# Two more MLP features as seven half-size products, and block masks by iota, in a two-layer encoder on one Trainium2 core

## The chip, the cores and the metric

The kernel runs on one core of a Trainium2 chip. The core has five engines that run side by side, each taking its own instructions in order: TensorE (PE in the profile; its weight loads are listed apart as PEld), VectorE (DVE), ScalarE (ACT), GpSimd (POOL) and SyncE (SP). They wait for each other through semaphores. Matrix products land in PSUM banks, everything else lives in SBUF. Loads are issued from the queue of SP, and some adding transfers from the queue of POOL; sixteen DMA engines move the data.

The metric is the device time of one execution, in microseconds. Smaller is better.

## The reference

The program is a two-layer encoder trunk on 512 tokens of width 1024, all in float32. Layer 0 mixes tokens with a bidirectional gated DeltaNet, layer 1 with a bidirectional gated linear attention (GLA). After each mixer and after each MLP the residual is normalised:

```python
for i in range(DEPTH):                       # DEPTH = 2
    m = _mixer_gdn(x, ...) if i == 0 else _mixer_gla(x, ...)
    x = _layernorm(ALPHA * x + m, ln1_g[i], ln1_b[i])
    x = _layernorm(ALPHA * x + _sq_relu_mlp(x, mlp_w1[i], mlp_w2[i]), ln2_g[i], ln2_b[i])

def _sq_relu_mlp(h, w1, w2):                 # w1: 1024 x 4096, w2: 4096 x 1024
    a = jax.nn.relu(jnp.matmul(h, w1))
    return jnp.matmul(a * a, w2)
```

The change touches the MLP, which is run twice, and the masks that the GLA layer uses to pick, level by level, which blocks of a score matrix come from which product.

## The kernel before

Every float32 operand of a large product is split into a high part `h` (a cast, on ACT, line 102) and a low part `l` (a subtraction, on DVE, line 107), and a product is three matmuls: high by high, high by low, low by high (lines 128 to 130). So every weight tile of 128 x 1024 costs one ACT cast and one DVE subtraction before PE can use it. The tiles are `wst` (as loaded), `wh` and `wl` (split); `wst` and the pair `wh`/`wl` are rings of three buffers each. A load can start when the split of the tile three places earlier is done, and a split can start when PE is done with the tile three places earlier.

The 4096 hidden features of the MLP form four groups of eight tiles of 128 features, here called features 1 to 8 of a group (the code counts from 0). The first product (with `w1`) makes a group's features, the second (with `w2`) adds a group's contribution to the output.

- **Group 0, features 1 to 4** (`proj_halves`): four full products, in two halves of 256 tokens.
- **Group 0, features 5 to 8** (`feature`): four full products of 512 tokens, 24 matmuls each.
- **Groups 1 to 3** (`Pair`): two features at a time. A 2 x 2 block product (two halves of the 1024 inputs by two halves of the tokens, for two features) is computed from seven half-size products instead of eight (a Strassen scheme), 12 matmuls of 256 tokens each. That needs sums of weight halves (line 464, DVE, and a half-size split, lines 470 and 471) and sums of token blocks of x (`x_blocks`, lines 433 to 442, then four more splits `xh3`, `xh5`, `xh6`, `xh7`). The x sums are made once for each MLP and used by all pairs.
- **The second product** (`second`) uses the same scheme with seven products for each group, in 28 pieces (`chunks`) of six matmuls of 512 columns. Its weight tiles are `w2r` (as loaded, eight buffers), `w2h` and `w2l`.

A pair's life: `begin` loads its two weight tiles t0 and t1 into `wst`; `prepare` splits t0 for products 1 and 2, forms the sums and splits half of one for product 5; `finish` (`late(0, ...)`) splits the rewritten t0 for products 6 and 4; `late(1, ...)` splits t1 for products 7 and 3, after the pair's second product. PE runs the products in the order 1, 2, 6, 5, 7, 3, 4. They accumulate in two PSUM banks, `fx` and `fyz`; these are the two buffers of the tag `pj`, which features 5 to 8 use too. Between the products ACT and DVE copy or add parts of the banks into the features `h`, and a product that adds to a bank waits until that copy has read it.

In groups 1 to 3 PE's order is written out by hand (`in_order`): pieces of the second product of group g stand between the products of the pairs of group g + 1. The order on DVE, ACT, POOL and SP is set by a scheduler, from priorities and its own estimate of when things end. The queues are then fixed: an instruction that waits holds up everything behind it on its engine.

The masks (`sel_masks`) are seven 128 x 128 tiles of bytes, made once, on POOL, during the first MLP: a memset, two selections, a subtraction and a cast for each level. They are first needed by the GLA layer. The line numbers of the profile are those of this kernel.

## Time and profile before

| what | value |
|---|---|
| median of the runs shown | 1311.15 us (1310.5 to 1313.33, 3 runs) |
| the profiled execution's own time | 1311.28 us |
| its span in the trace | 1309.6 us |
| PE busy | 1289.4 us, 98% of the span |
| DVE busy | 1106.3 us, 84% |
| ACT busy | 804.8 us, 61% |
| POOL busy | 134.6 us, 10% |
| features 5 to 8 of group 0, first MLP | 431.92 to 453.97 us on PE |
| features 5 to 8 of group 0, second MLP | 1005.01 to 1027.09 us on PE |

How to read it: a matmul's row gives its start and its length, but matmuls overlap, so what one costs is the distance from one start to the next. The same holds on DVE and ACT, where one instruction begins shortly before the one ahead of it has ended. "Idle before" in square brackets is the time that an engine stood still before an instruction, with what released it.

### The profile page before, as it was taken

Reading aid. Unit: us, or ns where it says so; the run is one execution under the profiler, and the core shown is the slowest. Engines: PE = TensorE matmul, PEld = TensorE weight load, DVE = VectorE, ACT = ScalarE, POOL = GpSimd, SP = SyncE. Lnnn points to the kernel's source line nnn. Section 1 sums busy time; section 2 is a strip of 40 time slices with the busy share of each in tenths; the row PEclk is TensorE's granted clock in tenths of the full one; section 3 lists DMA queues with packets and bytes.
Section 4 is the critical chain, followed back from the end, with each engine's and each line's share of the span. In section 5 each row is a group of like instructions: output and inputs, shape, how many; then the busy total and the mean of one; then the engine's idle time right before and its main releaser. Section 6 shows DMA issues by size and latency. Waiting matters only on the chain.

```text
span 1309.6 us, 22228 instructions
## 1 busy us (share of the span) xinstructions
PE 1289.4 (98%) x8586; PEld 1106.3 (84%) x8586; DVE 1106.3 (84%) x1795; ACT 804.8 (61%) x1604; POOL 134.6 (10%) x190
## 2 busy tenths in 40 slices
PE   8999999999999999999999999999999999999996
PEld 6778888788878899999998888888888899999985
DVE  7888888988868998999989697877888789989987
ACT  5767676677543656666657754564456566666656
POOL 5000000000003710101102100000000001101021
PEclk9999999999999999999999999999999999999998
DMA  5333313233332664576647521211316376556565
GB/s 191 99 106 96 98 55 108 81 114 96 114 110 84 175 172 169 119 203 161 177 145 154 140 97 56 74 62 52 103 59 218 87 210 165 142 176 139 171 143 144
DMA packets 47805, 165.92 MB, mean 127 GB/s; under 512 B 5923, under 2 KB 6611, under 8 KB 47699
## 3 DMA queue, kind: packets, MB, share of 16 engines
q1 hardware_dynamic: 33603, 114.52, 25.8%
q0 software_dynamic: 13984, 49.95, 18.7%
q8 instruction: 67, 1.10, 0.3%
q14 instruction: 39, 0.32, 0.1%
q10 hardware_dynamic: 112, 0.03, 0.0%
HBM read 125.00 MB, written 2.65 MB: 97 GB/s over the span
## 4 chain that ended last, share of the span: by engine, by line
PE 91%; ACT 3%; DVE 3%; issue 1%; DMA 1%; SPq 0%; DVEq 0%; ACTq 0%
PE pjv L128 3%; PE pjv L129 3%; PE pjv L130 3%; PE pX L130 3%; PE pX L129 3%; PE fx L130 3%; PE fx L128 3%; PE fx L129 3%; PE pX L128 3%; PE m L1776 3%; PE fyz L128 3%; PE fyz L130 3%; PE fyz L129 3%; PE pY L129 2%; PE pY L130 2%; PE pY L128 2%
## 5 line engine op out<-in xcount | busy, mean ns | idle before, releaser
L102 ACT CAST wh<-wst 128x1024 fp32r<-128x1024 f32 x151 | 158.5, 1050 | 104.8 <-PE fyz L129 28.2
L107 DVE TENSOR_TENSOR wl<-wst,wh 128x1024 fp32r<-128x1024 f32 x149 | 183.2, 1232 | 40.3 <-ACT wh L102 40.2
L107 DVE TENSOR_TENSOR w2l<-w2r,w2h 128x1024 fp32r<-128x1024 f32 x92 | 111.5, 1222 | 21.6 <-ACT w2h L102 21.6
L102 ACT CAST w2h<-w2r 128x1024 fp32r<-128x1024 f32 x94 | 98.4, 1048 | 42.5 <-DMA w2r<-w2r 22.8
L415 POOL DMA_DIRECT2D w2r<-w2r x56 | 47.9, 887 | 492.9 <-DVE w2l L107 388.0
L464 DVE TENSOR_TENSOR wst<-wst 128x512 f32<-128x512 f32 x120 | 80.0, 687 | 0.8
L102 ACT CAST ah<-h 128x1024 fp32r<-128x1024 f32 x56 | 58.8, 1050 | 30.6 <-PE pY L129 12.0
L107 DVE TENSOR_TENSOR al<-h,ah 128x1024 fp32r<-128x1024 f32 x56 | 68.4, 1221 | 6.6 <-ACT ah L102 6.6
L130 PE MATMUL pX<-w2h,al 128*128 128x512 f32 x168 | 66.3, 394 | 0.0
L129 PE MATMUL pX<-w2l,ah 128*128 128x512 f32 x168 | 65.9, 392 | 0.0
L128 PE MATMUL pX<-w2h,ah 128*128 128x512 f32 x168 | 65.5, 390 | 0.0
L128 PE MATMUL pjv<-wh,xth 128*128 128x512 f32 x128 | 54.7, 428 | 0.0
L130 PE MATMUL fyz<-xh,wl 128*128 128x256 f32 x192 | 53.5, 278 | 0.0
L130 PE MATMUL fx<-xth,wl 128*128 128x256 f32 x192 | 53.4, 278 | 0.0
L128 PE MATMUL fyz<-xh,wh 128*128 128x256 f32 x192 | 53.4, 278 | 0.0
L128 PE MATMUL fx<-xth,wh 128*128 128x256 f32 x192 | 53.2, 277 | 0.0
L130 PE MATMUL fx<-xh,wl 128*128 128x256 f32 x192 | 53.2, 277 | 0.0
L129 PE MATMUL fx<-xtl,wh 128*128 128x256 f32 x192 | 53.2, 277 | 0.0
L129 PE MATMUL fyz<-xl,wh 128*128 128x256 f32 x192 | 53.1, 277 | 0.0
L129 PE MATMUL fx<-xl,wh 128*128 128x256 f32 x192 | 53.1, 277 | 0.0
L128 PE MATMUL fx<-xh,wh 128*128 128x256 f32 x192 | 53.1, 277 | 0.0
L129 PE MATMUL pj<-xtl,wh 128*128 128x256 f32 (+1 forms) x160 | 52.0, 326 | 0.2 <-DVE xtl L194 0.2
(542 smaller groups left out, 4312.7 us busy)
## 6 DMA issues: line engine op xcount, KB each, us to landing
wst<-in_w SPq DMA_DIRECT2D x68, 512.0 KB, 4.6
w2r<-in_w SPq DMA_DIRECT2D x60, 512.0 KB, 4.6
w2r<-w2r POOLq DMA_DIRECT2D x56, 512.0 KB, 5.7
wst<-in_a_in SPq DMA_DIRECT2D x31, 512.0 KB, 4.1
wst<-in_b_vr SPq DMA_DIRECT2D x16, 512.0 KB, 3.3
wst<-in_a_out SPq DMA_DIRECT2D x8, 512.0 KB, 4.6
wst<-in_b_in SPq DMA_DIRECT2D x8, 512.0 KB, 3.4
wst<-in_b_out SPq DMA_DIRECT2D x8, 512.0 KB, 3.2
```

The lines of the kernel that those rows point to most:

```text
L102: h = nc.scalar.copy(hi, src)
L107: self.halves = h, nc.vector.tensor_tensor(lo, src, hi.bitcast(F32), ALU.subtract)
L128: mm(ps, ah, bh, start=start, stop=False, **kw)
L129: mm(ps, ah, bl, start=False, stop=False, **kw)
L130: self.last_mm = mm(ps, al, bh, start=False, stop=stop, **kw)
L415: nc.gpsimd.dma_start(blocks[a + (q,)], blocks[b + (q,)], accum_op=ALU.add)
L464: plus = lambda a, b: V.tensor_tensor(a, a, b, ALU.add)
L1776: T.matmul(ps[:, d, :], *ops(d), start=True, stop=True)
```

## The change

Three edits.

1. **Features 7 and 8 of group 0** are made as a pair, by the seven half-size products, in both MLPs. The x sums and their splits, which stood from feature 6 on, are asked for from feature 5 on. Nothing of the second product stands between this pair's products: they follow each other directly on PE. PE's written-out order starts at this pair and runs to the end of the MLP's last group. All later pairs move up by one place in the list `todo`.
2. **The masks** are made from iotas on POOL (one of 128 x 7, seven of 128 x 128) and comparisons on DVE (six shifts and a cast on 128 x 7, seven comparisons of 128 x 128). They move from the start of the first MLP to the end of its first round of groups. A mask of level k now marks every pair of positions that lies in different blocks of 2^k, not only those that first part at this level; the copies under the masks run from the finest level to the coarsest, and a later one overwrites an earlier one.
3. Two tiny memsets allocate the `w2h` and `w2l` rings at the place in the code where they were allocated before, so that the tiles' addresses stay what they were.

```diff
-        todo = [(gi, p) for gi in range(1, G) for p in range(GF // 2)]
+        todo = [(0, GF // 2 - 1)] + [(gi, p) for gi in range(1, G) for p in range(GF // 2)]
...
-        for f in range(4, GF):
+        def step(i, n):
+            if n == 0:
+                begin(i + 1)
+            elif n == 1:
+                ready[i].late(1, (7, 3))
+            elif n == 3:
+                prepare(i + 1)
+            elif n == 5:
+                finish(i + 1)
+
+        for f in (4, 5):
             feature(0, f, h)
-            if f >= 5:
-                next(xb)
-            if f == 4:
-                load(0, 0, 0)
-            if f == 5:
-                load(0, 0, 1)
-            if f == 6:
-                load(0, 1, 1)
-                with tc.issue_after(c.last_hi.ins), tc.issue_after(c.last_lo.ins):
-                    split(1)
-                a = pair(quarters(h)[0])
+            next(xb)
+            load(0, 0, f - 4)
         begin(0)
+        for name in RING["w2"][:2]:
+            V.memset(pool.tile([P, 2, 512], F32R, name=name, tag=name, bufs=3)[:, 0, 0:8].bitcast(F32), 0.0)
+        next(xb)
         prepare(0)
         finish(0)
-        if extra:
-            extra(lambda: pool.tile([P, P], F32, name="tmp", tag="tmp", bufs=2))
+        load(0, 1, 1)
+        with tc.issue_after(c.last_hi.ins), tc.issue_after(c.last_lo.ins):
+            split(1)
+        a = pair(quarters(h)[0])
+        whole = contextlib.ExitStack()
+        whole.enter_context(c.in_order(mybir.EngineType.PE))
+        for n, _ in enumerate(ready[0].products(h)):
+            step(0, n)
...
             h, a = nh, stream.a
+            if extra and gi == 0:
+                with tc.issue_after(c.halves[1].ins):
+                    extra(lambda: pool.tile([P, P], F32, name="tmp", tag="tmp", bufs=2))
...
 def sel_masks(c, pool, tmp):
...
+    G.iota(pi, pattern=[[0, n]], base=0, channel_multiplier=1)
+    for k in range(1, n):
+        V.tensor_scalar(pi[:, k:k + 1], pi[:, k:k + 1], k, None, ALU.arith_shift_right)
+    V.tensor_copy(pf, pi)
...
+    for k in range(n):
+        w = 1 << k
+        f = tmp()
+        G.iota(f.rearrange("p (a b) -> p a b", b=w), pattern=[[1, P // w], [0, w]], base=0, channel_multiplier=0,
+               allow_small_or_imprecise_dtypes=True)
+        m = out[w if k else 0] = pool.tile([P, P], mybir.dt.uint8, name=f"mu{w}", tag=f"mu{w}", bufs=1)
+        V.tensor_scalar(m, f, pf[:, k:k + 1], None, ALU.not_equal if k else ALU.is_equal)
```

On PE the order of all other matmuls stays as it was: in each MLP 48 matmuls of 512 columns go, and 84 of 256 come in their place. On the other engines the scheduler moved more. Three places matter.

**DVE, first MLP, the end of the preparation for the first pair.** In these rows `xl6`, `xl7` and `xl3` are splits of x sums, `wst_6052` is t0 and `wst_6054` is t1 of the first pair of group 1. The last row is the split for that pair's products 6 and 4. Before:

```order
L107 TENSOR_TENSOR xl6_6041<-w2r_5934,xh6_6040 128x1024
L107 TENSOR_TENSOR xl7_6045<-w2r_5938,xh7_6044 128x1024
L107 TENSOR_TENSOR xl3_6049<-w2r_5936,xh3_6048 128x1024
L107 TENSOR_TENSOR wl_6057<-wst_6052,wh_6056 128x1024
L464 TENSOR_TENSOR wst_6052<-wst_6052,wst_6054 128x512
L464 TENSOR_TENSOR wst_6054<-wst_6054 128x512
L464 TENSOR_TENSOR wst_6052<-wst_6052 128x512
L464 TENSOR_TENSOR wst_6052<-wst_6052,wst_6054 128x512
L107 TENSOR_TENSOR w2l_6150<-w2r_6135,w2h_6149 128x1024
L471 TENSOR_TENSOR wl_6064<-wst_6052,wh_6063 128x512
L464 TENSOR_TENSOR wst_6052<-wst_6052,wst_6054 128x512
L107 TENSOR_TENSOR wl_6070<-wst_6052,wh_6069 128x1024
```

Now, where `wst_5950` and `wst_5952` are t0 and t1 of the new pair (features 7 and 8 of group 0):

```order
L107 TENSOR_TENSOR xl6_5965<-w2r_5897,xh6_5964 128x1024
L107 TENSOR_TENSOR xl3_5973<-w2r_5899,xh3_5972 128x1024
L464 TENSOR_TENSOR wst_5950<-wst_5950,wst_5952 128x512
L107 TENSOR_TENSOR w2l_5998<-w2r_5905,w2h_5997 128x1024
L464 TENSOR_TENSOR wst_5952<-wst_5952 128x512
L464 TENSOR_TENSOR wst_5950<-wst_5950 128x512
L471 TENSOR_TENSOR wl_5984<-wst_5950,wh_5983 128x512
L464 TENSOR_TENSOR wst_5950<-wst_5950,wst_5952 128x512 x2
L107 TENSOR_TENSOR w2l_6002<-w2r_5907,w2h_6001 128x1024
L107 TENSOR_TENSOR al_6008<-h_5652,ah_6007 128x1024
L107 TENSOR_TENSOR wl_5990<-wst_5950,wh_5989 128x1024
```

The first split of the second product's weights (`w2l_5998`, `w2l_6002`) and of its left operand (`al_6008`) stood ahead of the rows shown before; they stand between the pair's own sums and its last split now.

**ACT, the same place.** `pj_5907` is feature 6 before, `w2h_6149` the cast of a later `w2` tile, and `wh_6069` the cast for products 6 and 4. Before:

```order
L383 ACTIVATE h_5653<-pj_5907 128x512
L384 ACTIVATE h_5653<-h_5653 128x512
L102 CAST w2h_6149<-w2r_6135 128x1024
L470 CAST wh_6063<-wst_6052 128x512
L383 ACTIVATE h_5653<-pj_5952 128x512
L384 ACTIVATE h_5653<-h_5653 128x512
L102 CAST wh_6069<-wst_6052 128x1024
```

Now, where `pj_5915` is feature 6 and `fx_6011` the first bank of the new pair:

```order
L470 CAST wh_5983<-wst_5950 128x512
L102 CAST w2h_6153<-w2r_6139 128x1024
L383 ACTIVATE h_5653<-pj_5915 128x512
L102 CAST wh_5989<-wst_5950 128x1024
L384 ACTIVATE h_5653<-h_5653 128x512
L499 COPY h_5653<-fx_6011 128x256
L102 CAST wh_6043<-wst_5952 128x1024
```

The cast of the later `w2` tile now stands ahead of the activation of feature 6, which empties the bank that the pair's second product needs. In the second MLP the same cast stands ahead of the activation of feature 5, and the cast for products 6 and 4 ahead of that of feature 6.

**DVE, first MLP, where the masks are made now.** These rows stand where the second product passes from group 0 to group 1; `wl_7030` is the split for products 7 and 3 of a pair. The comparisons for `mu32` and `mu64` follow within four more rows.

```order
L799 TENSOR_SCALAR pi_6923<-pi_6923 128x1 x6
L577 TENSOR_TENSOR h_6133<-h_6134,h_6133 128x4x256
L800 CAST pf_6924<-pi_6923 128x7
L107 TENSOR_TENSOR al_6984<-h_6134,ah_6983 128x1024
L503 TENSOR_TENSOR h_6967<-h_6967,fyz_6998 128x256
L808 TENSOR_SCALAR mu1_6935<-tmp_6933,pf_6924 128x128
L808 TENSOR_SCALAR mu2_6939<-tmp_6937,pf_6924 128x128
L107 TENSOR_TENSOR wl_7030<-wst_6760,wh_7029 128x1024
L808 TENSOR_SCALAR mu4_6943<-tmp_6941,pf_6924 128x128
L808 TENSOR_SCALAR mu8_6947<-tmp_6945,pf_6924 128x128
L107 TENSOR_TENSOR w2l_6992<-w2r_6975,w2h_6991 128x1024
L808 TENSOR_SCALAR mu16_6951<-tmp_6949,pf_6924 128x128
```

Before, no mask instruction stood on DVE. On POOL two of the iotas stay at the start of the MLP and five move behind the twelfth adding transfer of this MLP.

54 lines of the change are left out of this document (15 added, 39 removed).

## The prediction

> **What bounds the kernel now.** I read the busy shares and the chain of waits first, then the windows of the stage that the change touches.
>
> ```profile
> PE 1289.4 (98%) x8586; PEld 1106.3 (84%) x8586; DVE 1106.3 (84%) x1795; ACT 804.8 (61%) x1604; POOL 134.6 (10%) x190
> PE 91%; ACT 3%; DVE 3%; issue 1%; DMA 1%; SPq 0%; DVEq 0%; ACTq 0%
> 431.92:442.95 11.03, 11.03 (x51) 9.06 (x50) 11.03 (x10) 8.27 (x11) 10.20 (x13) 1.00 0.42 142
> 442.95:453.97 11.02, 11.02 (x49) 9.03 (x48) 9.95 (x11) 4.83 (x7) 7.67 (x9) 1.00 0.87 250
> 1005.01:1016.05 11.04, 11.04 (x50) 9.04 (x49) 6.79 (x6) 6.01 (x8) 1.70 (x2) 1.00 1.03 360
> 1016.05:1027.09 11.04, 11.04 (x49) 9.03 (x48) 6.33 (x8) 4.91 (x8) 0.00 (x0) 1.00 0.54 120
> ```
>
> The last four rows are features 5 and 6, then 7 and 8, of the first and of the second MLP: length, then the busy time of PE, PEld, DVE, ACT and POOL, the granted clock, the DMA share and GB/s. PE never stands still in them, at full clock, so fewer matmuls shorten these stretches as long as PE still never waits. DVE is as full as PE in the first MLP (11.03 of 11.03, 9.95 of 11.02) and has room in the second (6.79 and 6.33 of 11.04). So the question is whether the two stages can prepare a pair in time.
>
> **The matmuls: a gain of 2.95 us.** The starts on PE:
>
> ```profile
> 431.92 0.40 PE L128 MATMUL pj<-xth,wh 128*128 128x512 f32 x1
> ...
> 453.97 0.39 PE L128 MATMUL pX<-w2h,ah 128*128 128x512 f32 x1
> ...
> 455.36 0.28 PE L128 MATMUL fx<-xth,wh 128*128 128x256 f32 x1
> ...
> 456.72 0.28 PE L128 MATMUL fyz<-xth,wh 128*128 128x256 f32 x1
> ...
> 458.09 0.39 PE L128 MATMUL pX<-w2h,ah 128*128 128x512 f32 x1
> ...
> 1005.01 0.40 PE L128 MATMUL pj<-xth,wh 128*128 128x512 f32 x1
> ...
> 1027.09 0.39 PE L128 MATMUL pX<-w2h,ah 128*128 128x512 f32 x1
> ```
>
> Features 5 to 8 take 453.97 − 431.92 = 22.05 us, so two of them 11.03; in the second MLP 22.08, so 11.04. One half-size product takes 1.36 or 1.37 us (455.36 to 456.72 to 458.09), a mean of 1.365, so seven take 9.555. Each MLP saves 1.47 or 1.485 us, together 2.95.
>
> A rule speaks against that. The Trainium skill, TensorE: Matmul & The Clock Gate, section Back-to-back issue gap, gives a sustained spacing of about 81 ns for 128 columns and 131 ns for 512, so that narrow matmuls lose. An estimate by that page: 48 x 131 = 6.3 us go and at least 84 x 81 = 6.8 us come, a loss. The rows above do not agree (22.05 us / 96 = 230 ns for 512 columns, 1.365 us / 12 = 114 ns for 256, the same for each column).
>
> **First MLP: DVE comes too late by 1.6 us.** Before, the first pair's product 6 had two pieces of the second product between it and its preparation. Now the pair starts at 431.92 + 11.03 = 442.95, products 1 and 2 take 2.73, and the third matmul of product 6 needs the last DVE split of the new order on DVE (`wl_5990`): 442.95 + 2.73 + 2 x 0.114 = 445.9. When is it done?
>
> ```profile
> 421.94 1.22 DVE L433 TENSOR_TENSOR w2r<-xth,xtl 128x1024 f32<-128x1024 f32 x1
> ...
> 435.79 1.48 DVE L441 SCALAR_TENSOR_TENSOR w2r<-w2r 128x1024 f32<-128x1024 f32 x1
> ...
> 988.92 1.22 DVE L433 TENSOR_TENSOR w2r<-xth,xtl 128x1024 f32<-128x1024 f32 x1
> ...
> 1009.36 1.21 DVE L107 TENSOR_TENSOR xl<-w2r,xh 128x1024 fp32r<-128x1024 f32 x1
> ...
> 1019.81 2.75 DVE L464 TENSOR_TENSOR wst<-wst 128x512 f32<-128x512 f32 x4
> ...
> 545.86 1.29 DVE L464 TENSOR_TENSOR wst<-wst 128x512 f32<-128x512 f32 x2
> ```
>
> DVE can start the x sums at 421.94, when the last part of x is there, as before. From there to `wl_5990` DVE's queue now has 19 instructions of 1024 columns and six of 512. The second MLP shows the price with POOL quiet: from 988.92 to 1009.36 are 18 steps without a gap, 1.136 us each (in the first MLP, beside the masks on POOL, such an instruction took up to 1.48 instead of 1.22; those masks are gone). The 512-wide ones take 0.64 (1.29 / 2) to 0.69 (2.75 / 4) by their lengths. So the end is at 421.94 + 18 x 1.136 + 1.22 + 6 x 0.64 to 0.69 = 447.4 to 447.75, if nothing on DVE waits. PE waits 1.5 to 1.85 us; with one or two short waits of DVE for ACT inside this walk, or the 512-wide ones at the closer spacing that back-to-back rows hide, 1.3 to 2.0. I take 1.6. This eats the first MLP's 1.47.
>
> **ACT ahead of the banks: 0.2 and 0.4 us.** In both MLPs the pair's casts now stand directly before the activations and copies that free a bank.
>
> ```profile
> 450.27 1.05 ACT L102 CAST w2h<-w2r 128x1024 fp32r<-128x1024 f32 x1 [5.16 <-DMA w2r<-in_w]
> ...
> 1016.33 1.05 ACT L102 CAST w2h<-w2r 128x1024 fp32r<-128x1024 f32 x1 [3.67 <-DMA w2r<-in_w]
> 1017.28 1.04 ACT L102 CAST wh<-wst 128x1024 fp32r<-128x1024 f32 x1
> 1018.24 0.59 ACT L383 ACTIVATE h<-pj 128x512 f32<-128x512 f32 x1
> ```
>
> Second MLP: the cast for products 6 and 4 needs feature 6's weight buffer, free at 1016.05; it ends at 1017.1, and the activation of feature 6 behind it at 1017.7. Product 2 wants that bank at 1016.05 + 1.365 = 1017.4: 0.3 us late. Product 3 waits for a copy behind another cast for about 0.1. The split itself is done by 1017.1 + 1.22 = 1018.3, and product 6 needs it at 1016.05 + 2.96 = 1019.0: no wait there, and DVE is free by then (988.92 + 25.8 = 1014.7). So the second MLP keeps 1.485 − 0.4 = 1.1 us. In the first MLP the same copies cost about 0.2.
>
> **Loads.** The next pair's t1 can be loaded only when t0's buffer is free, that is after `wl_5990` (447.5), and DVE wants it at about 452.7, when product 7 is done (447.5 + 1.1 + 2 x 1.365 = 451.3) and a split and an addition behind it: 5.2 us. In the second MLP: 1018.3 to 1024.5, 6.2 us. Issues and landings:
>
> ```profile
> w2r<-in_w SPq DMA_DIRECT2D x4, 512.0 KB, 4.9
> ...
> w2r<-in_w SPq DMA_DIRECT2D x4, 512.0 KB, 8.7
> ...
> 443.63 2.79 SPq L52 DMA_DIRECT2D w2r<-in_w  x3
> ...
> 1008.33 2.60 SPq L52 DMA_DIRECT2D w2r<-in_w  x2
> ```
>
> The first two rows are the median landing times from 425 to 460 and from 995 to 1035. 4.9 us fits, 8.7 would not; in the second MLP 8.7 went with two adding transfers at the same time (DMA share 1.03 above), and these now start later, behind the moved `w2l` splits. I take 0.2 us for the first MLP, none for the second; the far end is 8.7 in both: 3.5 and 2.5 us.
>
> **Masks: 0.3 us.** On POOL a mask cost, before, two selections, a subtraction and a cast, off the path:
>
> ```profile
> L796 POOL TENSOR_SCALAR_AFFINE_SELECT tmp<-tmp 128x128 f32<-128x128 f32 x7 | 7.9, 1134 | 0.3
> ...
> 409.91 0.15 DVE L206 TENSOR_SCALAR rst<-rst 128x1 f32<-128x1 f32 x1
> ...
> 459.65 0.41 DVE L503 TENSOR_TENSOR h<-h,fyz 128x256 f32<-128x256 f32 x1
> ...
> 542.05 1.22 DVE L107 TENSOR_TENSOR wl<-wst,wh 128x1024 fp32r<-128x1024 f32 x1 [0.65 <-ACT wh L102]
> ...
> 548.00 1.29 DVE L464 TENSOR_TENSOR wst<-wst 128x512 f32<-128x512 f32 x2
> ...
> 550.61 1.05 ACT L102 CAST wh<-wst 128x1024 fp32r<-128x1024 f32 x1 [0.99 <-PE fx L129]
> ...
> 551.91 0.28 PE L128 MATMUL fx<-xth,wh 128*128 128x256 f32 x1
> 552.03 0.28 PE L129 MATMUL fx<-xtl,wh 128*128 128x256 f32 x1
> ```
>
> Removing them from the path costs and brings nothing but the quieter DVE counted above. The new work on DVE is seven tiny instructions (0.15 or less) and seven of 128 columns, between 0.15 and 0.41, say 0.27: 2 to 3 us. An iota does not stand in the trace; the nearest row of its size on POOL is the selection, 1.13 us, the memset beside it 0.2. Five iotas each wait for a comparison to free one of two buffers, so at 1.1 us each DVE waits up to 2 us more. What is behind: the sums of line 464, done at 549.3 before, of which ACT's cast at 550.61 had no need before PE freed its buffer. So about 1.3 us of lateness is free; another 1.1 comes from an `al` split that now stands behind these sums, and 0.65 from the gap at 542.05. Cost: 0 to 2 us, taken as 0.3.
>
> **The sum**, against the profiled execution's 1311.28 (span 1309.6 and 1.7 around it; the median of the runs is 1311.15, 0.13 below): −2.95 + 1.6 + 0.2 + 0.4 + 0.2 + 0.3 = −0.25 us. On the median that is **1310.9 us**: no change. By the low ends (1.3 and 0.3 for the ACT waits, nothing else) 1309.8; by 2.0 for DVE, 0.6 for ACT and 2 for the masks, with 0.2 for loads, 1313.0.
>
> **Rivals.**
>
> 1. *The whole gain arrives* (1308.2): PE does not wait, because the last split is not needed where I put it or DVE is quicker. For it: PE never waited in these stretches before. Against it: 25 instructions in a fixed order on DVE do not fit into the 24.0 us from 421.94 to 445.9. Chance 0.12.
> 2. *A load stops ACT* (slower). The place is the cast of the later `w2` tile, which waited 5.16 and 3.67 us for its load before, when nothing behind it was urgent. Now the activation that frees the pair's bank is behind it. The load is issued when `xl6` is done, the 14th long instruction on DVE, so at about 438.0 in the first MLP and 1005.3 in the second. It decides from a landing time of about 5.6 us on in the first MLP. With 8.7: landed 446.7, cast to 447.75, activation to 448.35, but product 2 wants the bank at 444.3; 4.05 us, and 0.65 more for the split behind it, instead of 1.6: +3.1. Second MLP: landed 1014.0, then two casts and the activations, 1.4 us of waits instead of 0.4: +1.0. In all −0.25 + 4.1 = +3.9, 1315.0; with t1 late in both as well some 1320. For it: the 8.7 of the second MLP. Against it: fewer adding transfers at that time now. Chance 0.22.
> 3. *The masks hold DVE* by their full bound, and the moved copies with it: 1310.9 + 1.7 = 1312.6 by the bounds above, over 1313.8 only if an iota takes about 2 us. Chance 0.05, nearly all of it counted as no change.
> 4. *Narrow matmuls are slower in a run of 84 without wide ones between.* The trace has no such run; at the 0.12 us of the two matmuls from 551.91 to 552.03, instead of 0.114, it is 84 x 0.006 = 0.5 us for each MLP, 1311.9. The page's rule named above goes the same way. Chance 0.03.
>
> **How the numbers follow.** A measurement of this kernel can tell about 0.2%, 2.6 us, from no change: below 1308.5 is faster, above 1313.8 slower. My forecast has a chance of 0.58. Faster takes rival 1 and little else: 0.12. Slower takes rival 2 and the far ends of loads and masks: 0.26. No change has 0.62. The likeliest case's own range is 1309.8 to 1313.0; with part of rivals 1 and 2 the range is 1308.7 to 1315.0.
>
> **What would show it right or wrong.** Right: in the first MLP PE waits once, at the third matmul of product 6, for DVE's `wl` of line 107, by 1.3 to 2.0 us; in the second only for short waits of `fyz` on ACT; one half-size product takes 1.365 us; DVE's long instructions from 422 to 447 take 1.22 us, not 1.3 and more. Wrong: PE without a wait there (rival 1), a wait of PE for ACT of over 2 us with ACT waiting for a `w2r` load ahead of it (rival 2), or PE idle between 545 and 555 (the masks).

## The result and the profile after

The changed kernel took 1315.75 us (median of 7 runs, 1314.78 to 1317.71) against 1311.27 us for the kernel before on the same chip: a ratio of 1.0035 [1.0026, 1.0044], 4.5 us more. That is slower by more than 0.2%, and outside the range of the prediction (1308.7 to 1315.0). Three executions on record took 2585 to 4523 us, in three kernels of which one is the kernel before; they are left out of all times, and the one profile taken in such an execution is not used.

The page of the profile after, with the busy times, the shares of the chain of waits, and the queue that brings TensorE's program:

```profile
PE 1290.3 (98%) x8658; PEld 1108.0 (84%) x8658; DVE 1115.6 (85%) x1833; ACT 808.4 (61%) x1616; POOL 109.4 (8%) x163
PE 81%; DVE 8%; ACT 5%; DMA 4%; issue 2%; POOL 0%; SPq 0%; DVEq 0%; ACTq 0%; POOLq 0%
q8 instruction: 68, 1.11, 0.3%
```

PE's busy time grew by 0.9 us (1289.4 to 1290.3) and the span by 6.3 (1309.6 to 1315.9): nearly all of the lost time is waiting. In the chain of waits PE fell from 91% to 81%, DVE rose from 3% to 8% and DMA from 1% to 4%. The windows of the four stretches that the prediction worked with (features 5 and 6, then the new pair, in the first and in the second MLP; columns as there):

```profile
433.30:444.49 11.19, 11.19 (x51) 9.23 (x51) 11.19 (x13) 8.98 (x13) 0.94 (x1) 1.00 0.70 232
444.49:455.80 11.31, 10.37 (x85) 9.92 (x84) 10.07 (x14) 6.90 (x12) 1.75 (x2) 1.00 0.79 191
1011.77:1022.82 11.05, 11.05 (x50) 8.94 (x49) 10.53 (x13) 7.16 (x11) 2.62 (x3) 1.00 0.93 257
1022.82:1032.89 10.07, 10.07 (x86) 9.75 (x85) 5.55 (x8) 5.77 (x10) 0.86 (x1) 1.00 0.93 220
```

The pair takes 11.31 us in the first MLP (11.02 before) and 10.07 in the second (11.04 before): +0.29 and −0.97, −0.68 together. The pairs are not where the kernel got slower. The loss lies in stretches whose matmuls did not change. PE's waits of over 0.15 us from the pair to the end of the second mixer's stage, apart from five of 0.17 to 0.68 us that stand in both kernels:

```profile
448.83 0.39 PE L130 MATMUL fx<-xh,wl 128*128 128x256 f32 x1 [0.94 <-DVE wl L107]
488.00 0.39 PE L128 MATMUL fx<-xh,wh 128*128 128x256 f32 x1 [0.34 <-ACT h L506]
498.50 0.38 PE L128 MATMUL fyz<-xth,wh 128*128 128x256 f32 x1 [0.55 <-ACT h L523]
572.15 0.39 PE L128 MATMUL fx<-xth,wh 128*128 128x256 f32 x1 [0.17 <-DVE h L513]
577.71 0.38 PE L128 MATMUL fyz<-xth,wh 128*128 128x256 f32 x1 [1.15 <-ACT h L523]
948.59 0.70 PE L1079 MATMUL stp<-v,kdt 128*128 128x256 f32 x2 [1.31 <-ACT kdt L1069]
```

The kernel before has none of these six. A wait costs more than its number, since the rows of matmuls overlap: behind the 0.94 at 448.83, product 6 takes 1.35 us longer.

The rest is read from one table. An entry says by how much more the start of the same matmul lags the kernel before at the end of a stretch than at its beginning (us; times are those of the kernel before; the last row is what follows PE's last product, so that a column adds up to the difference of the spans). "Again" is the changed kernel once more; its first 100 us do not have the 1.4 us that the first profile lost there, so its column is the better one for sizes. The other columns are experiments, told below.

| stretch | after | again | masks alone | pair in 2nd MLP alone | before, fetch moved | masks late | masks late, fetch moved |
|---|---|---|---|---|---|---|---|
| start to 440 | +1.56 | −0.43 | −0.11 | −0.65 | +1.46 | −0.16 | −0.17 |
| 440 to 460, first pair | +0.26 | +0.29 | 0 | 0 | 0 | +0.30 | +0.29 |
| 460 to 500 | +1.41 | +1.36 | 0 | 0 | +0.55 | +1.36 | 0 |
| 500 to 580 | +1.93 | +2.24 | +1.73 | 0 | 0 | 0 | 0 |
| 580 to 930 | −0.07 | −0.19 | −0.11 | 0 | +0.01 | −0.14 | 0 |
| 930 to 1000 | +1.55 | +1.35 | 0 | −0.11 | +0.79 | +1.05 | −0.04 |
| 1000 to 1030, second pair | −0.90 | −0.86 | 0 | −0.90 | 0 | −0.85 | −0.92 |
| 1030 to 1300 | −0.09 | −0.24 | −0.03 | +1.76 | +0.66 | +0.10 | −0.44 |
| last transfers | +0.65 | +0.68 | +0.02 | +0.20 | +0.13 | +0.64 | +0.68 |
| span against 1309.6 | +6.3 | +4.2 | +1.5 | +0.3 | +3.6 | +2.3 | −0.6 |

So four pieces explain the result: 1.4 us at 460 to 500, 1.9 to 2.2 at 500 to 580, 1.3 to 1.5 at 930 to 1000, and 0.65 behind the last product. Against them stand about 0.6 us that the two pairs gain.

**460 to 500 and 930 to 1000: PE's program arrives in the middle of a transfer.** ACT's casts ahead of the waits at 498.50 and 948.59, first after, then before:

```profile
486.63 1.05 ACT L102 CAST w2h<-w2r 128x1024 fp32r<-128x1024 f32 x1 [3.72 <-DMA w2r<-w2r]
947.01 1.04 ACT L102 CAST wh<-wst 128x1024 fp32r<-128x1024 f32 x1 [2.73 <-DMA wst<-in_w]
```

```profile
482.62 1.05 ACT L102 CAST w2h<-w2r 128x1024 fp32r<-128x1024 f32 x1 [2.02 <-DMA w2r<-w2r]
939.60 1.05 ACT L102 CAST wh<-wst 128x1024 fp32r<-128x1024 f32 x1 [0.36 <-DMA wst<-in_w]
```

The same casts wait 1.7 and 2.4 us longer for their transfers. The view of the DMA engines over 7 us, in 40 slices of 0.175 us, shows what such a transfer looks like. After, 941 to 948, with one row of its queues:

```profile
GB/s 0 0 0 0 0 0 0 0 211 164 164 257 398 421 374 398 398 117 0 0 0 23 0 0 23 0 23 47 23 23 23 0 0 0 0 0 0 0 0 0
q8 instruction: 1, 0.02, 0.9%
```

Before, 934 to 941, the same load:

```profile
GB/s 187 47 0 0 0 0 0 0 0 0 0 0 0 0 0 0 0 0 0 234 328 211 421 328 351 351 421 258 94 0 0 0 0 0 0 0 0 47 0 0
```

In both, the load of 512 KB moves at up to 421 GB/s and is nearly done after ten slices. After, single packets follow for another 2.3 us: 23 GB/s in a slice of 0.175 us is one packet of 4 KB. The tail holds eight of them (six slices of 23 and one of 47), a sixteenth of the load's 128, so it looks like the share of one of the sixteen engines. In that window the queue q8 has one piece of 16 KB: 0.9% of 16 engines over 7 us, that is 1.0 us of one engine (it lies between 943.5 and 944). After, 485 to 490 (slices of 0.125 us), the same tail stands behind the adding transfers of line 415, with a piece of q8 between 484 and 484.5:

```profile
GB/s 328 131 229 197 229 262 98 229 229 197 229 197 164 262 0 66 0 0 33 0 33 0 0 33 0 33 393 98 229 295 33 360 131 164 328 66 295 197 66 393
```

Queue q8 is TensorE's program: 8658 matmuls, each with a weight load, are 17,316 instructions in 68 pieces, about 255 for a piece. PE takes one every 19 us on average. The Trainium skill, Runtime: NRT & Kernel Launch, section Instruction fetch mechanics, has it so: the program comes in blocks of 16 KiB, 256 instructions, over the sequencer's own DMA queue, and the cost is "mostly hidden". The count agrees; "hidden" holds for PE itself, which shows no gap, but not for the transfers that ACT waits for, 1.7 to 2.4 us longer here. The 36 matmuls that the new pair has more in the first MLP are 72 instructions: they moved the piece that came after 487 us, between transfers, forward into the transfer that ACT waits for. The 18 usable profiles of this case, all kernels told below among them, agree on the second place. On the clock of the kernel before, seven of them have a piece of q8 that starts between 937.3 and 938.8, and there the cast of 939.60 waits 1.52 to 2.73 us; in the other eleven it waits 0.34 to 0.50.

**500 to 580: the masks' work comes ahead of two splits that have no room.** On DVE and POOL after, the masks' rows, then the splits behind them and the transfer that they release:

```profile
536.81 0.45 DVE L799 TENSOR_SCALAR pi<-pi 128x1 int32<-128x1 int32 x6
539.85 0.47 DVE L808 TENSOR_SCALAR mu<-tmp,pf 128x128 uint8<-128x128 f32 x2
541.38 0.47 DVE L808 TENSOR_SCALAR mu<-tmp,pf 128x128 uint8<-128x128 f32 x2
542.91 0.47 DVE L808 TENSOR_SCALAR mu<-tmp,pf 128x128 uint8<-128x128 f32 x2
543.90 0.27 DVE L808 TENSOR_SCALAR mu<-tmp,pf 128x128 uint8<-128x128 f32 x1
552.49 1.21 DVE L107 TENSOR_TENSOR al<-h,ah 128x1024 fp32r<-128x1024 f32 x1
553.63 2.35 DVE L107 TENSOR_TENSOR w2l<-w2r,w2h 128x1024 fp32r<-128x1024 f32 x2
555.61 1.76 POOL L415 DMA_DIRECT2D w2r<-w2r  x2 [12.08 <-ACT h L523]
```

Before:

```profile
544.39 1.22 DVE L107 TENSOR_TENSOR al<-h,ah 128x1024 fp32r<-128x1024 f32 x1
549.20 2.35 DVE L107 TENSOR_TENSOR w2l<-w2r,w2h 128x1024 fp32r<-128x1024 f32 x2
551.17 1.72 POOL L415 DMA_DIRECT2D w2r<-w2r  x2 [14.39 <-DVE w2l L107]
```

The two `w2l` splits free the raw tiles, so POOL's adding transfer can start: in both kernels it does so about 0.75 us after the first split's end (the row after names ACT, but this distance is the same). They come 4.43 us later than before, while PE at that time lags by 3.24, so the transfers are late by 1.2 us. That is the masks' work: by the distances of the starts it takes 1.81 us on DVE (with a cast at 538.31), and DVE had 0.65 us of idle time there before (ahead of the split at 542.05, a row of the prediction), which is gone. The `al` split stands ahead of the `w2l` splits in both kernels. It moved from ahead of the sums of line 464 to behind them, which brings these sums back to PE's lag, but nothing for the `w2l` splits. The casts wait for the transfers, the activations of line 523 stand behind the casts, and PE waits 1.15 us for one of them at 577.71.

**The last 0.65 us.** The profile's last 8 us in 40 slices, after and before:

```profile
GB/s 389 389 410 348 348 205 410 348 369 123 338 369 379 379 358 348 430 420 379 348 328 358 399 389 389 389 379 92 61 20 20 0 0 0 0 0 0 0 0 0
q14 instruction: 2, 0.02, 0.5%
```

```profile
GB/s 0 205 410 369 389 389 389 348 174 369 389 369 133 348 399 307 358 379 348 410 389 399 410 307 359 399 369 359 420 369 226 0 0 0 0 0 0 0 0 0
```

The same picture: a tail of single packets behind the output, and two pieces of another instruction queue, q14, in the window. In all 18 usable profiles of this case the stretch from the end of DVE's last instruction to the end of the span is 4.3 to 4.5 us without such a piece (5 of them), 4.4 to 4.6 with one (4; 5.0 in a fifth) and 5.0 with two (8). In all nine at 5.0 a piece starts 3.1 to 3.2 us before the end, in none of the others; but these nine are also all the kernels with the pair in both MLPs. No run moved that piece alone, so this does not tell the piece from the rest of the change.

### The profile page after: what moved, and what is told of

The parts are those of the page before. It is cut to its first block, busy times and chain, and to the rows that moved or that the text cites. A ratio compares the mean times of both kernels' runs of the same rounds, so it can differ in the third digit from the quotient of the medians.

```text
span 1315.9 us, 22386 instructions
## 1 busy us (share of the span) xinstructions
PE 1290.3 (98%) x8658; PEld 1108.0 (84%) x8658; DVE 1115.6 (85%) x1833; ACT 808.4 (61%) x1616; POOL 109.4 (8%) x163
## 4 chain that ended last, share of the span: by engine, by line
PE 81%; DVE 8%; ACT 5%; DMA 4%; issue 2%; POOL 0%; SPq 0%; DVEq 0%; ACTq 0%; POOLq 0%
PE pjv L128 3%; PE pjv L129 3%; PE pjv L130 3%; PE m L1777 3%; PE pX L130 3%; PE pX L129 3%; PE pX L128 3%; PE fx L130 3%; PE fx L128 3%; PE fx L129 3%; PE fyz L128 2%; PE fyz L130 2%; PE fyz L129 2%; DMA w2r<-w2r 2%; PE scp L1009 2%
## 5 line engine op out<-in xcount | busy, mean ns | idle before, releaser
L464 DVE TENSOR_TENSOR wst<-wst 128x512 f32<-128x512 f32 x130 | 86.1, 684 | 0.9 <-DMA wst<-in_w 0.5
L130 PE MATMUL fx<-xh,wl 128*128 128x256 f32 x208 | 57.6, 277 | 0.9 <-DVE wl L107 0.9
L128 PE MATMUL fx<-xh,wh 128*128 128x256 f32 x208 | 57.8, 278 | 0.3 <-ACT h L506 0.3
L128 PE MATMUL fyz<-xh,wh 128*128 128x256 f32 x208 | 58.0, 279 | 0.0
L130 PE MATMUL fyz<-xh,wl 128*128 128x256 f32 x208 | 57.9, 278 | 0.0
L128 PE MATMUL fx<-xth,wh 128*128 128x256 f32 x208 | 57.7, 277 | 0.2 <-DVE h L513 0.2
L130 PE MATMUL fx<-xth,wl 128*128 128x256 f32 x208 | 57.8, 278 | 0.0
L129 PE MATMUL fx<-xtl,wh 128*128 128x256 f32 x208 | 57.6, 277 | 0.0
L129 PE MATMUL fyz<-xl,wh 128*128 128x256 f32 x208 | 57.5, 277 | 0.0
L130 PE MATMUL pjv<-wh,xtl 128*128 128x512 f32 x128 | 50.2, 392 | 0.0
```

The source lines that it names most:

```text
L128: mm(ps, ah, bh, start=start, stop=False, **kw)
L129: mm(ps, ah, bl, start=False, stop=False, **kw)
L130: self.last_mm = mm(ps, al, bh, start=False, stop=stop, **kw)
L464: plus = lambda a, b: V.tensor_tensor(a, a, b, ALU.add)
```

## The experiments

Matmuls that are added write a bank that nothing reads. A ratio is against the kernel before, timed beside it.

**The changed kernel again.** No edit.

> The changed kernel once more, unaltered: a second profile of it. Its first profile stands 6.3 us of span behind the kernel before, in pieces: +1.4 in the first 40 us, +0.5 in the first pair, +0.5 and +0.8 between 480 and 500 (ACT waits 2.2 and 3.7 us for an adding transfer ahead of its cast), +0.5 and +1.4 between 560 and 578, +1.6 in the second attention stage, -0.8 in the second pair, -0.25 behind. Theory A (the pieces from the pair on belong to the change): the pieces between 480 and 578 come again within 0.5 us each; the 1.4 at the start, where both kernels issue the same, does not. Theory B (the length of the adding transfer at 481, 5.8 us instead of 4.1, is chance): the piece at 480 to 500 falls below 0.4 us. Time 1314.8 to 1317.

Measured: 1315.54 us, 1.0029 [1.0017, 1.0041]. The loss repeats, and so do its pieces (second column of the table).

**The pair with the old masks.** The selections on POOL, with their call at the old place, and both pairs:

```diff
+        if extra:
+            extra(lambda: pool.tile([P, P], F32, name="tmp", tag="tmp", bufs=2))
         a = pair(quarters(h)[0])
...
-            if extra and gi == 0:
-                with tc.issue_after(c.halves[1].ins):
-                    extra(lambda: pool.tile([P, P], F32, name="tmp", tag="tmp", bufs=2))
```

> The pair in both MLPs, with the block masks made as before (by selections on POOL), asked for where the kernel before asks for them. Theory 1 (the loss comes from the pair in the first MLP, whose late work pushes what follows): +4 to +5 us against the kernel before, 1315 to 1316.5, with ACT's long waits for adding transfers at 480 to 490 and 555 to 570 as in the changed kernel. Theory 2 (the loss comes from the masks at their new place: comparisons on DVE, the a-split behind them, and another order of loads on SP): +0.5 for the pair, minus 1 for the second MLP, so -0.5 to +1, 1310.8 to 1312.3, and the adding transfer at about 550 starts no later than PE is behind there.

Measured: 1316.39 us, 1.0039 [1.0026, 1.0051]. The pair's waits on PE, and one of the x sums on DVE:

```profile
445.54 0.38 PE L128 MATMUL fyz<-xth,wh 128*128 128x256 f32 x1 [1.48 <-ACT h L383]
448.25 0.39 PE L128 MATMUL fx<-xh,wh 128*128 128x256 f32 x1 [1.03 <-ACT h L499]
449.88 0.39 PE L130 MATMUL fx<-xh,wl 128*128 128x256 f32 x1 [1.12 <-DVE wl L107]
...
430.13 1.49 DVE L440 TENSOR_TENSOR w2r<-w2r 128x1024 f32<-128x1024 f32 x1
```

The changed kernel's row for that sum:

```profile
431.45 1.22 DVE L440 TENSOR_TENSOR w2r<-w2r 128x1024 f32<-128x1024 f32 x1
```

With the selections on POOL a long DVE instruction takes up to 1.49 us instead of 1.22, and the first pair costs +3.3 us instead of +0.3. Two of the waits are for ACT, which itself stood waiting for DVE's sums and for a load. So taking the masks away from there is worth 3 us to the pair. The piece at 500 to 580 is absent here, so the pair doesn't make it; that at 460 to 500 stays (+1.39). At 930 to 1000 it loses only 0.34: the cast there waits 1.52 us for its load.

**The masks alone.** The kernel before with the new masks at their new place, without the pair:

```diff
-        if extra:
-            extra(lambda: pool.tile([P, P], F32, name="tmp", tag="tmp", bufs=2))
...
+            if extra and gi == 0:
+                with tc.issue_after(c.halves[1].ins):
+                    extra(lambda: pool.tile([P, P], F32, name="tmp", tag="tmp", bufs=2))
```

> The kernel before with only the masks changed: iotas and comparisons, asked for after the first round of the groups; features 7 and 8 stay ordinary. Theory 1 (pair): no change, 1310.6 to 1312. Theory 2 (masks): +1.9 us between 550 and 578 (adding transfers start 1.3 us or more later than before, ACT's casts behind them, PE waits for ACT's copies and activations), 1313 to 1315; if the order of SP's loads is what moves the transfer at 480 too, another +1.3.

Measured: 1313.71 us, 1.0018 [1.0009, 1.0027]; the span grows by 1.5, and all of it lies at 570 to 580:

```profile
574.16 0.39 PE L128 MATMUL fyz<-xth,wh 128*128 128x256 f32 x1 [1.16 <-ACT h L523]
```

The `w2l` splits start at 550.28 here, 1.08 us later than before with PE 0.12 ahead: again 1.2. The masks alone make this piece, with PE's program as it was, and no other.

**The pair in the second MLP alone.** The first MLP and the masks are those of the kernel before (a copy of the old function is called for it).

```diff
-            mlp(c, a["w1_0"], a["w2_0"], ...
+            mlp_first(c, a["w1_0"], a["w2_0"], ...
```

> The first MLP as in the kernel before, masks too; only the second MLP's features 7 and 8 are the pair. All theories: the gain of the second pair that the changed kernel's trace shows, -0.8 us (forecast: -1.1), and no loss, so 1310.0 to 1310.8. If the 1.6 us lost in the attention stage between the two MLPs and whatever is lost behind the second pair come here too, they are not the first MLP's: 1311.5 or more.

Measured: 1312.37 us, 1.0006 [0.9997, 1.0015]. The second pair gains its 0.90 us, and the rest of the second MLP gives 1.76 back. Only one wait of over 0.15 us stands there (0.20). But 46 of the 91 half-size products in this MLP take over 1.39 us without a wait, against 26 of 84 before and 8 of 91 after; the mean is 1.402 instead of 1.381 in each of these two, so 91 x 0.021 = 1.9 us. By the tiles' addresses in the program, 24 of the slow ones have their high weights in the middle place of the `wh` ring while the low ones aren't in the middle of `wl`; most of the others (18) have the high ones in the first place and the low ones in the last.

**The two weight rings moved by one place each, on top of that.** A tile is skipped in `wl` once, and in `wh` once:

```diff
-    def side_by_side(self, st, n):
+    def side_by_side(self, st, n, skip="wl"):
...
+        nc.vector.memset(self.wtile(skip, [P, 1, 8])[:, 0, :].bitcast(F32), 0.0)
...
-        specs = [(c.side_by_side(gst, 32), "gps", "ac")]
+        specs = [(c.side_by_side(gst, 32, "wh"), "gps", "ac")]
```

> The pair in the second MLP alone, and one tile of the weight rings skipped ahead of each attention stage (a low tile in the first, a high tile in the second, each written with 8 zeros), so that a product's high and low weights lie in other places. In the traces a half-size product takes 1.41 us instead of 1.365 where the high weights lie in the middle place of the ring and the low ones do not: 24 products in each MLP before, some 38 in the second MLP of the kernel with the pair there alone. Theory R (the place sets it): no product above 1.39 without a wait; the first MLP 1.1 us shorter, the second 1.1 shorter and 0.9 more for the pair: 1308.0 to 1309.2. Rival (it is what happens beside them): products stay at 1.41 in half the pairs, 1311.5 to 1312.5.

Measured: 1311.67 us, 1.0004 [0.9995, 1.0013]: level with before. Slow products without a wait: 10 of 91, the mean 1.389; in the first MLP 3 of 84, where the kernel before has 24. None and 1308.0 to 1309.2 us had been expected: the first MLP became only 0.24 us shorter (440 to 930), not 1.1. Two successive products (fx, then fyz) with nothing between, before and in this kernel:

```profile
1039.54 0.28 PE L128 MATMUL fx<-xh,wh 128*128 128x256 f32 x1
...
1042.37 0.39 PE L128 MATMUL pZ<-w2h,ah 128*128 128x512 f32 x1
```

```profile
1038.90 0.28 PE L128 MATMUL fx<-xh,wh 128*128 128x256 f32 x1
...
1041.63 0.39 PE L128 MATMUL pZ<-w2h,ah 128*128 128x512 f32 x1
```

2.83 us against 2.73. So where the weights lie in SBUF decides whether such a product is slow; why is open. The 0.7 us between the medians of these two kernels is not told apart by their intervals, and 0.75 us is still given back after 1030, with waits of PE for line 523 (957 in this kernel; 0.22 twice) among it.

**Moving PE's program.** If a fetch in a transfer is what costs, matmuls added ahead of everything must move the loss without anything else changing. First by small f32 products behind the 20 idle transposes at the start, 36 in the kernel before and 92 in the changed one:

```diff
             for i in range(20):
                 nc.tensor.transpose(idle[:, i % NT, :], c.ident, c.ident)
+            for i in range(36):
+                nc.tensor.matmul(idle[:, i % NT, :4], c.ident, c.ident[:, :4], start=True, stop=True)
```

> The kernel before, with 36 matmuls of 4 columns added behind the 20 that idle at the start, their results unused; nothing else changes. PE then takes its 16 KB pieces of program 36 matmuls earlier, as in the changed kernel behind the first pair (84 - 48 = 36 more matmuls). Theory F (in the changed kernel such a piece falls into the adding transfer of about 475 to 483 and into the load of about 937 to 943, and one DMA engine brings the rest of the transfer late): beside a shift at the start, PE falls behind by 1.0 to 1.4 us between 476 and 500 (ACT's cast waits 3.6 us for the adding transfer instead of 2.0) and by 0.3 to 1.5 at about 942, with no pair in the program. Rival L (the pair's own lateness on ACT and DVE lengthens what follows): none of it, the offset stays flat from 100 us to the end within 0.3.

> The changed kernel with 92 matmuls of 4 columns added at the start, their results unused: 36 + 92 = 128 matmuls, one whole piece of program, so PE fetches behind the first pair at the same places in the work as the kernel before. Theory F: the loss of 1.35 us between 476 and 500 and that of 1.3 at about 942 are gone (below 0.3 each); the 0.5 and 1.45 us at 560 to 578 stay; the start costs some us more, which is read from the offset at 100 us. Rival L: both losses stay.

Measured: 1324.16 us (1.0098) and 1349.31 us (1.0292); 13.7 and 35.6 us of that are the added products themselves, about 0.4 us each, ahead of the first MLP. In the kernel before, the shift missed the place that was named: nothing at 460 to 500 and 930 to 1000, but +0.8 at 640 to 660, with a piece of q8 at 646 in an adding transfer. The trace has two matmuls for each such f32 product (8658 instead of 8586), so it moves the program by more instructions than the two that I had assumed. In the changed kernel both pieces are gone and only the masks' wait is left:

```profile
518.99 1.05 ACT L102 CAST w2h<-w2r 128x1024 fp32r<-128x1024 f32 x1 [1.99 <-DMA w2r<-w2r]
977.01 1.05 ACT L102 CAST wh<-wst 128x1024 fp32r<-128x1024 f32 x1 [0.50 <-DMA wst<-in_w]
...
610.04 0.39 PE L128 MATMUL fyz<-xth,wh 128*128 128x256 f32 x1 [1.17 <-ACT h L523]
```

The two casts wait as before (2.02 and 0.36).

Then the other direction, the kernel before made to lose, with more of the same transposes (36 and 42 more, one execution of each; the edit shown is the second):

```diff
-            for i in range(20):
+            for i in range(62):
                 nc.tensor.transpose(idle[:, i % NT, :], c.ident, c.ident)
```

> The kernel before with 56 idle transposes at the start instead of 20, nothing else. The 36 matmuls of 4 columns tried before shifted the program's pieces on PE by some 15 us instead of 5.6, past the adding transfer; a transpose of this kind stands in the program once, as the pair's matmuls do, so the piece that the kernel before fetches at 488 should come at about 482 (counted without the shift at the start). Theory F (code fetch meets the adding transfer): PE loses 1.0 to 1.4 us between 476 and 500 there, with a tail of 12 to 35 GB/s in the transfer. Against it: flat within 0.3 although the fetch lies at 481 to 484.

> The kernel before with 62 idle transposes at the start instead of 20. With 56 the piece of program came at 483.5, 1.1 of them the shift of the start, when the third adding transfer (landed at 483.75) was all but done; six matmuls more bring it 0.7 to 0.9 us earlier, into the transfer. Theory F: PE loses 1.0 to 1.4 us between 476 and 500, with no pair in the program, and ACT's cast waits 3.6 us for the adding transfer instead of 2.0. Rival L (that loss belongs to the pair): flat within 0.3 there.

Measured: 1314.73 and 1314.87 us. With 36 the fetch came at 483.61, when the adding transfer was all but done (the cast behind it starts at 483.75 and nothing is lost there), and it hit the load at 940: +1.2 us. With 42 it hit both:

```profile
485.36 1.05 ACT L102 CAST w2h<-w2r 128x1024 fp32r<-128x1024 f32 x1 [3.25 <-DMA w2r<-w2r]
943.20 1.05 ACT L102 CAST wh<-wst 128x1024 fp32r<-128x1024 f32 x1 [1.95 <-DMA wst<-in_w]
```

This kernel has neither pair nor new masks, and it loses 0.55 and 0.79 us where the changed one does. So the fetch alone makes these waits; with the fetch moved away, as above, they are gone. It doesn't give the full 1.36 of the first place: in the changed kernel the earlier cast there waited longer too (2.17 against 1.68), so ACT had less slack. That this makes the other 0.8 is argued, not shown.

**The same with short products.** To move the program with less time added, products of 16 columns in bf16, on top of the kernel with the pair in the second MLP and the rings moved: 8, 4 and 2 transposes with 44, 80 and 114 of them (the edit shown is the third).

```diff
-            for i in range(20):
+            for i in range(2):
                 nc.tensor.transpose(idle[:, i % NT, :], c.ident, c.ident)
+            half = c.ident.bitcast(BF16)
+            for i in range(114):
+                nc.tensor.matmul(idle[:16, i % NT, :16], half[:, :16], half[:, :16], start=True, stop=True)
```

> The kernel with the pair in the second MLP alone and the rings shifted, whose idle matmuls at the start are 8 transposes and 44 matmuls of 16 columns in bf16 instead of 20 transposes: 32 more instructions pairs ahead of everything. The work is the same, only the places in it at which PE fetches a piece of its program move, by about a quarter of a period. Theory F: the offsets against the kernel before change in steps of 0.2 to 1.4 us at transfers on which ACT waits, at other places than without the shift; the sum moves by up to 2 us either way. Rival: the offsets follow those of the kernel without the shift within 0.3 behind the start, 1311.7.

> The same with 4 transposes and 80 matmuls of 16 columns: 64 more, half a period. Theory F: another set of steps, 1308.5 to 1313; rival: as without the shift, 1311.7.

> The same with 2 transposes and 114 matmuls of 16 columns: 96 more, three quarters of a period. Theory F: another set of steps, 1308.5 to 1313; rival: as without the shift, 1311.7.

Measured: 1312.06 us, 1.0006 [0.9996, 1.0015]; 1314.09, 1.0020 [1.0010, 1.0029]; 1313.40, 1.0015 [1.0005, 1.0025]. None beats the kernel before. The traces of the first and the third already lag by 1.1 and 1.25 us at 100 us, and the third has two more waits of PE for ACT (0.39 at 1060 and 0.54 at 1070.5); of the second only the time is used. Behind 1030 the first loses 0.02 us and the third 1.03, where the same kernel without the shift loses 0.75. So a place for the program that is good for one transfer is not good for all.

**The masks without their order.** The masks are asked for at once instead of behind `c.halves[1]`; the scheduler then puts them at 410 to 421 us, before the x sums:

```diff
             if extra and gi == 0:
-                with tc.issue_after(c.halves[1].ins):
-                    extra(lambda: pool.tile([P, P], F32, name="tmp", tag="tmp", bufs=2))
+                extra(lambda: pool.tile([P, P], F32, name="tmp", tag="tmp", bufs=2))
```

> The changed kernel, with the masks asked for at the same line but not told to wait for the second product's split: their iotas and comparisons then stand ahead of the x sums, at about 410 us, and behind it every engine has the order that it has with the old masks. Theory M (it is not the masks' 2 us of DVE work but the order around them: the a-split ahead of the two splits that release the adding transfers, 1.1 us, and a cast of weights ahead of ACT's cast): the loss of 1.7 to 1.9 us at 560 to 578 is gone, the pieces at 480 to 500 and 942 stay: 1313.5 to 1314.2. Rival W (the work itself costs): DVE's x sums start 2 us later and the first pair with them, 1315 to 1316.

Measured: 1315.84 us, 1.0035 [1.0023, 1.0048]. The piece at 500 to 580 is gone (the `w2l` splits start 3.53 us later than before, which is PE's lag), but 1.8 us are lost by 440 us instead, where DVE waits for iotas:

```profile
416.04 1.06 DVE L807 TENSOR_SCALAR mu<-tmp,pf 128x128 uint8<-128x128 f32 x2 [0.68 <-POOL tmp L804]
...
420.23 0.48 DVE L807 TENSOR_SCALAR mu<-tmp,pf 128x128 uint8<-128x128 f32 x2 [0.81 <-POOL tmp L804]
```

Then the masks are asked for two rounds of groups later than in the change, the smallest edit of all:

```diff
-            if extra and gi == 0:
+            if extra and gi == 2:
```

> The changed kernel with the masks asked for after the third round of the groups instead of the first, behind that round's split as before; no other instruction changes its place against the kernel with the old masks. Theory M (the order around the masks): no loss at 560 to 578 (flat within 0.3 where the changed kernel loses 0.8 + 1.45), the rest as in the changed kernel; 1313.4 to 1314.2 unless the end of the first MLP pays for the 2 us of DVE work. Rival W (the work): the same 1.7 us or more at about 700, 1315 to 1316.

Measured: 1313.71 us, 1.0018 [1.0009, 1.0028]; 1.8 to 2.0 us less than the two medians of the change, all of it at 500 to 580, where the lag now stays at 1.50 us. Its DVE and POOL:

```profile
543.55 1.23 DVE L107 TENSOR_TENSOR wl<-wst,wh 128x1024 fp32r<-128x1024 f32 x1 [0.65 <-ACT wh L102]
550.70 2.36 DVE L107 TENSOR_TENSOR w2l<-w2r,w2h 128x1024 fp32r<-128x1024 f32 x2
...
552.69 1.74 POOL L415 DMA_DIRECT2D w2r<-w2r  x2 [15.39 <-DVE w2l L107]
```

DVE's 0.65 us of idle time is there again, the `w2l` splits start 1.50 us later than before, as PE does, and at 551.17 + 1.50 = 552.67 the adding transfer is where it was. The masks' instructions are as many as in the change; at their new place, 682 to 687, nothing is lost. So it is the place of the work that cost the time: there, the splits behind it had no room.

**Both mended.** Late masks, and 92, 60 or 52 short products behind the 20 transposes to move PE's program:

```diff
-            if extra and gi == 0:
+            if extra and gi == 2:
...
+            half = c.ident.bitcast(BF16)
+            for i in range(52):
+                nc.tensor.matmul(idle[:16, i % NT, :16], half[:, :16], half[:, :16], start=True, stop=True)
```

> The whole change with both losses taken away: masks after the third round, and 92 small matmuls (16 columns, bf16, results unused) behind the idle transposes at the start, so that behind the first pair PE fetches its program at the places of the kernel before (36 + 92 = 128 matmuls, a whole piece). If pair, masks' order and fetches are all there is, the offset against the kernel before goes, counted from 100 us on: +0.3 in the first pair, nothing at 476 to 500, 560 to 578 and 942, -0.9 in the second pair, -0.3 to +0.2 behind; -0.6 to -1.1 in all. The start costs 0.5 to 1.5, so 1310.6 to 1312. If something else is in the loss, the sum stays above +0.5.

> As the whole change with masks after the third round and small idle matmuls, but 60 of them instead of 92: every fetch of program on PE some 5 us later in the work. Theory F: nothing at 476 to 500, 560 to 578 and 942, -0.9 in the second pair, and the 1.4 us lost behind it (at 1060 to 1090, 1126 to 1150 and 1210 to 1240) shrink to 0.3 or less: -0.6 to -1.1 us against the kernel before, 1309.8 to 1310.5. If the second MLP's losses belong to the pair, they stay: 1311.5 or more.

> The same with 52 small idle matmuls, another 1.2 us later. Theory F: as with 60, or with other steps of 0.2 to 0.8 us where a fetch now meets another transfer: 1309.8 to 1311. If the losses belong to the pair, 1311.5 or more.

Measured: 1312.54 us, 1.0009 [0.9999, 1.0019]; 1312.22, 1.0008 [0.9999, 1.0017]; 1311.09, 0.9998 [0.9989, 1.0007]. In all three the pieces at 460 to 580 and 930 to 1000 are gone. With 92, a fetch at 1126 falls into another adding transfer (the cast at 1129.94 waits 3.40 us instead of 1.97). All three came out above what their pieces had promised (1309.8 to 1310.5 for 60); behind 1030 the first two lose 1.35 and 0.92 us. With 52, none falls into one that matters, and the two casts wait as before:

```profile
483.17 1.05 ACT L102 CAST w2h<-w2r 128x1024 fp32r<-128x1024 f32 x1 [1.99 <-DMA w2r<-w2r]
939.69 1.05 ACT L102 CAST wh<-wst 128x1024 fp32r<-128x1024 f32 x1 [0.44 <-DMA wst<-in_w]
```

Its matmuls end 1.28 us ahead of the kernel before, and the last transfers take 0.68 of that back: span −0.6, and the time cannot be told from no change. No version beat the kernel before by more than its measurement is uncertain.

## Why the prediction was right and where it failed

**The matmuls, −2.95: right.** On PE the third, fourth and fifth products of the new second pair start at 1025.86, 1027.22 and 1028.58, 1.36 us apart with no gap, so a run of narrow matmuls is not slower in itself; the longer ones of this pair (1.46 to 1.57 us) stand where the next product needs a bank that a copy must have read; that this makes them longer is argued, not shown. That takes away rival 4 and the rule of the Trainium skill named beside it (TensorE: Matmul & The Clock Gate, Back-to-back issue gap): the trace has 114 ns for 256 columns in the long run as well.

**The waits in the pairs: right in sum.** Seven products at 1.365 are 9.555 us; the first pair took 11.31, so 1.75 us of waits where 1.6 + 0.2 were predicted. PE waits at the third matmul of product 6 for `wl` of line 107, as said, for 0.94 us, which costs 1.35; the banks cost 0.4 instead of 0.2. How the sum divides differs from profile to profile. In the second one the pair takes as long (11.33), but the bank comes late first:

```profile
444.27 0.39 PE L128 MATMUL fyz<-xth,wh 128*128 128x256 f32 x1 [0.19 <-ACT h L383]
446.83 0.39 PE L130 MATMUL fx<-xh,wl 128*128 128x256 f32 x1 [0.34 <-DVE wl L107]
```

Products 1 and 2 lose 0.4 us each there and product 6 only 0.8. The matmul that needs the split starts 4.34 us behind the pair's start in the first profile and 4.33 in the second, so what the bank takes ahead of it is not lost again. Neither wait reaches the 1.3 to 2.0 us that were named as the sign. The second pair lost 0.51 instead of 0.4. DVE's long instructions take 1.22 us with POOL quiet, as assumed. The pair by itself, −2.95 + 1.6 + 0.2 + 0.4 = −0.75, measured −0.68. Rival 1 did not happen. Rival 2's chain is what the 0.19 us above shows, small: the cast of the later `w2` tile waits 2.79 us for its load, until 442.67, and the activation that frees the bank stands behind it. The load was issued at 437.52, so it landed within 5.2 us, under the 5.6 from which the rival counted. The 0.2 us for loads did not show either.

**The masks, +0.3: wrong by what stands behind them.** Measured +1.73 alone and 1.9 to 2.2 in the change. The work was no larger than predicted: 1.81 us on DVE instead of 2 to 3, and at this place no wait for an iota. The step that failed is the sentence on what is behind. It names the sums of line 464 alone, and counts 1.3 us of lateness against ACT's cast at 550.61, 1.1 us from the `al` split that moved behind them, and the idle 0.65 us as free. For the sums this held: they end 0.05 us behind PE's lag. But the 1.1 us are free only for what `al` was moved behind. The two `w2l` splits still stand behind `al` and behind all of the masks' work, so of the 1.81 us only the 0.65 were free for them, and they release POOL's adding transfers, ACT's casts and, over line 523, PE. I did not ask what each pushed-back instruction releases on the other engines. Rival 3 had the size, 2 us, with a chance of 0.05; its mechanism, DVE waiting for iotas, shows in the variant with early masks (0.68 and 0.81 us).

**What no term had: PE's program.** Of the 4.2 us in the second profile, 1.36 + 1.35 come where a fetch falls into a transfer, and 0.68 in the last transfers. The prediction counted 36 more matmuls for each MLP as time alone; that their instructions move the places where the program is fetched was put at nothing, without a reason. The sum without that, with the masks' term as measured, is −0.25 − 0.3 + 1.9 = +1.35, a time of 1312.5: still "no change". The fetches made it slower.

**What stays open:** why a product is slower with its weights at one place in the rings; what makes the other 0.8 us at 460 to 500; and whether the 0.65 us at the end is the pieces of q14, which the tail suggests and no run tested.

## What to carry to other kernels

When an edit puts work into an engine's queue, follow what every instruction behind it releases on the other engines to the end, transfers included; the lateness that one of them can bear says nothing of the next. An edit that changes the number of instructions on a full engine also moves the places where its program is fetched: look in the profile for the instruction queue's pieces inside transfers that something waits for, and compare a change at two or three places of the program before its last microsecond is believed.

## What the runs showed of the hardware

- A fetch of 16 KB of PE's program takes about 1 us of one DMA engine, and the cast behind a transfer of 512 KB in flight at that time waits 1.2 to 2.4 us longer (3.25 to 3.72 us instead of 2.02, and 1.52 to 2.73 instead of 0.36). PE itself shows no gap at that moment.
- The same half-size product took 1.41 us instead of 1.365 according to where its weight tiles lay in SBUF (46 of 91 such products were slow, 10 of 91 after the rings had been moved).
- A PE wait of 0.94 to 1.16 us cost 1.35 to 1.45 us in the starts behind it.
